# Fourier tables made and kept in the Fourier stage; the next layer's norm woven with the last out-projection

## The chip, the cores and the metric

The kernel runs on one core of a Trainium2 chip. The metric is the device time of one execution in microseconds (us). The core has a matmul engine (PE), a vector engine (DVE), a scalar engine (ACT), a general engine (POOL) and a sync engine (SP) that issues most of the DMA transfers. Each engine takes its own instructions in order; they meet through semaphores.

## The reference

Two layers of an encoder over 1040 tokens (16 learned ones and 1024 given) of width 1024. In one layer:

```
hn   = rmsnorm(h, norm_w[i])
proj = hn @ w_in[i]                      # all groups' inputs and gates
y_fft = real(fft2(u_fft, ortho)) @ fourier_w[i] * silu(g_fft)
y_pool, y_ssd, y_att = ...               # pooling, two-way state-space scan, attention
h    = h + concat(y_pool, y_fft, y_ssd, y_att) @ w_out[i]
```

The two-dimensional transform is done as matmuls with cosine and sine tables. The inner ones run over the 512 channels. Because `fourier_w` follows directly, the kernel first multiplies the channel tables with `fourier_w` (the "Fourier tables" of this text: four of 128x512 and one row of 512), and then multiplies the folded input with those.

## The kernel before

All activations stand with channels on the 128 partitions and tokens along the free dimension, in three token chunks of 348, 346 and 346. Float32 products are made from three matmuls on values split in a high part `hh` and a low part `hl` (`mm3`, L132 to L135; the split itself, L128 to L130, is an ACT copy and a DVE subtraction). A pool of 30 buffers called `big` holds almost everything of full length.

A layer runs so. `prenorm` (L156) loads the eight tiles of h from DRAM, squares them on ACT, sums them on POOL, DVE and in a matmul with ones (L175), takes the root (`rstd`), multiplies (L180) and splits (L181, L182). `att_kv` (L546) projects keys and values, and its evacuation (`qk_chunk`, L526) needs the cosine and sine tables of the rotary by DMA. `fft_tables` (L389) loads `cc`, `cn` and four blocks of `fw` by DMA; the blocks 1 and 3 come as 127 rows, since their first row is loaded apart (L402, L403). It adds and subtracts them (L407, L411), multiplies (L415, L417), copies the results out (L419) and writes them to DRAM. Then come the query projections and the four attention heads-pairs (`att_q`, `att_max`, `att_main`), with all other projections woven between them as "fill". After that come the Fourier stage (`fft_inner`, L423, `fft_outer`, L474, `fft_mix`), which loads the tables and the folded input back from DRAM and splits them, and the backward and forward scans; the out-projections of the groups (`outproj`, L320) are the fill here. Each step of `outproj` reads a 128x346 piece of the running h from DRAM (`ht`, L328), adds 12 matmuls to it (L337) and writes it to DRAM again (L338). The last out-projection runs for chunks 0 and 1 beside the forward scan and for chunk 2 alone (L1047, L1049).

`weave` and `stage` (L956, L1024) set in which order the program is written; a scheduler then orders each engine's instructions and gives the buffers out. Nearly all DMAs stand in SP's one queue, in the order in which SP issues them. `ps` gives out the PSUM banks: in the attention the ring for the out-projection ("mm") has three, the ring for small sums ("xx") one.

Of the kernel before, what the change touches and what calls it, by code (L numbers as in the profile page):

```python
# [12 lines left out]
F32R = mybir.dt.float32r  # L13
# [6 lines left out]
D = 1024  # L20
# [32 lines left out]
def hybrid_trunk(ctx: ExitStack, tc: tile.TileContext, io, out, depth=DEPTH):  # L53
# [36 lines left out]
    TE = nc.vector  # L90
    PN, PG, TB = ((2, 2, 8), ((0, 2, 4, 6), (0, 3, 6), (1, 3, 5)), 3)
# [59 lines left out]

    def vec(l, col, n=1):
        return vecs[:, l * NV + col:l * NV + col + n]


    def prenorm(l, s, src):  # L156
        h = [big() for _ in range(8)]
        hh = s.hh = [big(F32R) for _ in range(8)]
        hl = s.hl = [big(F32R) for _ in range(8)]
        for ci, (c0, cw) in enumerate(CH):  # L160
            for d in range(8):
                nc.sync.dma_start(h[d][:, c0:c0 + cw], src(d, ci))
        for ci, (c0, cw) in enumerate(CH):
            ss = ps("xx")
            n = PN[ci]
            for i in range(n):
                eng = (nc.gpsimd, nc.vector)[i % 2]
                for d in range(i, 8, n):
                    sq = chunk_tile("pl" if d == i else "pf")
                    nc.scalar.activation(sq[:, :cw], h[d][:, c0:c0 + cw], AF.Square)  # L170
                    if d == i:
                        acc = sq
                    else:
                        eng.tensor_tensor(acc[:, :cw], acc[:, :cw], sq[:, :cw], op=ALU.add)
                nc.tensor.matmul(ss[:, :cw], ones, acc[:, :cw], start=(i == 0), stop=(i == n - 1))  # L175
            rs = rstd(ss[:, :cw], cw, D)
            for d in range(8):
                t = sm()
                hi, lo = hh[d][:, c0:c0 + cw], hl[d][:, c0:c0 + cw]
                nc.vector.scalar_tensor_tensor(t[:, :cw], h[d][:, c0:c0 + cw], vec(l, V_NW + d), rs[:, :cw], op0=ALU.mult, op1=ALU.mult)  # L180
                nc.scalar.copy(hi, t[:, :cw])  # L181
                (nc.gpsimd if d in PG[ci] else nc.vector).tensor_tensor(lo, t[:, :cw], f(hi), op=ALU.subtract)  # L182
            yield
# [33 lines left out]

    def win(l, t):
        return wsplit([wraw(io["w1"][l, t, :, 4 * i:4 * i + 4]) for i in range(2)])
# [935 lines left out]
```

## Time and profile before

| | |
|---|---|
| median of 3 runs | 2183.52 us (2173.6 to 2186.84) |
| profiled execution | 2183.98 us, of it 2181.9 us span |
| PE busy | 2002.1 us, 92% |
| DVE, ACT, POOL busy | 1323.7, 1004.6, 642.0 us |
| mean granted PE clock | 0.964 |

An engine's share is an average over stages. PE is nearly full in the attention stages; what matters here is the three kinds of place where it is not: the start of each layer, the making of the Fourier tables, and the Fourier stage and the scans.

### The profile page before, as it was taken

To read this page: it belongs to the slowest core of one execution; us is meant where nothing else is said; L and a number is where in the kernel's file an instruction comes from. 1 tells how busy PE (TensorE), PEld (TensorE's weight loads), DVE (VectorE), ACT (ScalarE), POOL (GpSimd) and SP (SyncE) were. 2 spreads that over 40 slices of the span, in tenths; PEclk is the share of its full clock that TensorE was granted. 3 is DMA by queue.
4 is the path that set the end of the run, shared out by engine and by line. 5 is a ranking of instruction groups with operands and counts; after the bars stand their busy time and mean duration, and the time that the engine had idled before them with its cause. 6 is when DMAs were issued, how large, how long until landed. Compare 5 with 4: busy or idle time off the path is not lost. (4 is left out here: it accounts for less than half of the span.)

```text
span 2181.9 us, 33618 instructions
## 1 busy us (share of the span) xinstructions
PE 2002.1 (92%) x11868; PEld 1755.1 (80%) x11868; DVE 1323.7 (61%) x2614; ACT 1004.6 (46%) x2191; POOL 642.0 (29%) x642
## 2 busy tenths in 40 slices
PE   6699999989999999988976999999999999988888
PEld 5498888867899868877864988888778997878778
DVE  6373535558566355689864735256576554466996
ACT  5335254444443456346443353444435425463562
POOL 3005235135131220245220142441442304112550
PEclk9799999999999999999997999999999999999999
DMA  4321222113224478776743212121223335776666
GB/s 131 103 86 61 59 66 74 36 56 95 94 81 137 126 217 267 195 186 187 223 125 108 88 59 68 64 63 34 76 81 99 124 113 149 246 231 179 176 190 188
DMA packets 170374, 269.48 MB, mean 124 GB/s; under 512 B 21522, under 2 KB 117334, under 8 KB 170206
## 3 DMA queue, kind: packets, MB, share of 16 engines
q1 hardware_dynamic: 167550, 258.01, 39.0%
q0 software_dynamic: 2656, 9.33, 1.7%
q8 instruction: 93, 1.52, 0.3%
q14 instruction: 75, 0.61, 0.1%
HBM read 189.27 MB, written 73.77 MB: 121 GB/s over the span
## 5 line engine op out<-in xcount | busy, mean ns | idle before, releaser
L133 PE MATMUL psmm<-big,wh 128*128 128x346 f32 (+2 forms) x1920 | 639.8, 333 | 27.0 <-ACT sms L334 9.2
L134 PE MATMUL psmm<-big,wh 128*128 128x346 f32 (+2 forms) x1920 | 629.7, 328 | 7.7 <-DVE big L130 4.0
L135 PE MATMUL psmm<-big,wl 128*128 128x346 f32 (+2 forms) x1920 | 626.3, 326 | 2.0 <-DVE wl L130 2.0
L646 POOL TENSOR_TENSOR acc<-acc,pf 116x346 f32<-116x346 f32 (+4 forms) x336 | 343.9, 1048 | 531.6 <-ACT pf L637 531.5
L133 PEld LDWEIGHTS psmm<-big,wh 128*128 128x128 f32 x1920 | 367.9, 192 | 62.2 <-issue 21.7
L134 PEld LDWEIGHTS psmm<-big,wh 128*128 128x128 f32 x1920 | 368.2, 192 | 19.5 <-DVE big L130 8.4
L135 PEld LDWEIGHTS psmm<-big,wl 128*128 128x128 f32 x1920 | 368.3, 192 | 6.3 <-DVE wl L130 2.6
L130 DVE TENSOR_TENSOR wl<-wr,wh 128x512 fp32r<-128x512 f32 x232 | 182.8, 792 | 215.2 <-ACT wh L129 214.2
L129 ACT CAST wh<-wr 128x512 fp32r<-128x512 f32 (+1 forms) x236 | 145.0, 616 | 270.9 <-PE psmm L134 216.7
L133 PE MATMUL psy<-big,wh 128*128 128x346 f32 (+2 forms) x672 | 224.1, 334 | 0.0
L134 PE MATMUL psy<-big,wh 128*128 128x346 f32 (+2 forms) x672 | 223.1, 332 | 1.1 <-POOL big L182 0.7
L135 PE MATMUL psy<-big,wl 128*128 128x346 f32 (+2 forms) x672 | 219.2, 326 | 0.0
L606 DVE TENSOR_REDUCE mx<-psy 128x1 f32<-128x346 f32 (+3 forms) x272 | 132.8, 512 | 56.1 <-PE psy L605 55.4
L637 ACT ACTIVATE pf<-psy 116x346 f32<-116x346 f32 (+4 forms) x288 | 125.6, 457 | 80.3 <-PE psy L635 77.2
L656 PE MATMUL pspv<-pf,vt 116*64 116x346 f32 (+5 forms) x864 | 160.6, 463 | 0.0
L133 PEld LDWEIGHTS psy<-big,wh 128*128 128x128 f32 x672 | 129.9, 193 | 10.9 <-issue 8.8
L134 PEld LDWEIGHTS psy<-big,wh 128*128 128x128 f32 x672 | 130.0, 193 | 8.5 <-DVE big L130 2.8
L135 PEld LDWEIGHTS psy<-big,wl 128*128 128x128 f32 x672 | 130.3, 194 | 1.3 <-issue 0.8
L606 DVE TENSOR_REDUCE mx<-pssc 128x1 f32<-128x346 f32 (+3 forms) x136 | 69.9, 514 | 69.3 <-PE pssc L605 68.4
L337 DVE TENSOR_TENSOR sms<-sms,psmm 128x346 f32<-128x346 f32 (+2 forms) x128 | 65.1, 511 | 73.7 <-PE psmm L135 43.8
L656 PEld LDWEIGHTS pspv<-pf,vt 116*64 116x64 f32 (+1 forms) x864 | 58.6, 136 | 61.5 <-issue 24.0
L634 PE MATMUL psy<-big,big 128*116 128x346 f32 (+4 forms) x288 | 95.8, 334 | 8.1 <-DVE mx L606 7.2
(285 smaller groups left out, 3331.3 us busy)
## 6 DMA issues: line engine op xcount, KB each, us to landing
wr<-w SPq DMA_DIRECT2D x248, 256.0 KB
hd<-sms SPq DMA_DIRECT2D x112, 173.0 KB
sms<-hd SPq DMA_DIRECT2D x112, 173.0 KB
bb<-csd SPq DMA_DIRECT2D x40, 338.0 KB
md<-big SPq DMA_DIRECT2D x24, 520.0 KB
gd<-sms SPq DMA_DIRECT2D x64, 173.0 KB
big<-gd SPq DMA_DIRECT2D x16, 520.0 KB
big<-md SPq DMA_DIRECT2D x16, 520.0 KB
```

Source lines behind the costliest of these rows:

```text
L129: nc.scalar.copy(hi, src)
L130: nc.vector.tensor_tensor(lo, src, f(hi), op=ALU.subtract)
L133: nc.tensor.matmul(out_ps, ah, bh, start=start, stop=False)
L134: nc.tensor.matmul(out_ps, ah, bl, start=False, stop=False)
L135: nc.tensor.matmul(out_ps, al, bh, start=False, stop=stop)
L337: nc.vector.tensor_tensor(ht, ht, p[:, :cw], op=ALU.add)
L606: nc.vector.tensor_reduce(mx[:qn, q, e, ci:ci + 1], p[:qn, :cw], axis=AX.X, op=ALU.max)
L634: nc.tensor.matmul(p[:n, :cw], k1[:, k0:k0 + n], s1[e][:, cs], start=True, stop=False)
L637: nc.scalar.activation(pf[:n, :cw], p[:n, :cw], AF.Exp, scale=0.125)
L646: nc.gpsimd.tensor_tensor(accs[c0, e][:n, :cw], accs[c0, e][:n, :cw], pf[:n, :cw], op=ALU.add)
L656: nc.tensor.matmul(hold["pv"][64 * e:64 * e + 64, :cw], s.vt[:n, k, v, :], pfs[e][:n, :cw], start=(k == 0), stop=(k == len(KTS) - 1))
```

## The change

The Fourier tables are no longer made between `att_kv` and the queries but at the start of the Fourier stage, as a generator of its own, with out-projection steps between its matmuls. They are split straight from PSUM and kept in SBUF; their way through DRAM (`md["t"]`) and the loads of them in `fft_inner` are gone. `prenorm` is now written per chunk with yields. In layer 0 the weights of keys and values are loaded behind the first chunk of x and before the other two; the norms of chunks 1 and 2 are woven with the key and value projections, and 12 steps of the fill with the last of these. The last out-projection of layer 0 writes its sums into SBUF tiles (`sink`) as well as to DRAM, so that layer 1 loads no h for its norm; the norms of its chunks 0 and 1 are woven with the out-projection of chunk 2, that of chunk 2 with the key and value projections. `ssd_parts` packs three chunks in one buffer. The numbers of fill steps move accordingly (`FB`, `FN`, `FK`).

```diff
-    FB = (6, 6, 0, 1, 4, 1, 6, 9)
+    FB = (5, 5, 4, 1, 4, 1, 6, 9)
     GA = (22, 23, 22, 13)
     PS, WF = 60, 1.5
-    FN = (10, 17, 17, 17, 28)
+    FK = 3
+    FN = (9, 17, 17, 16, 27)
...
+    PN, PG = ((8, 2, 8), (2, 2, 8)), ((0, 2, 4, 6), (0, 3, 6), (1, 3, 5))
...
+    def load_h(s, src, ci):
+        c0, cw = CH[ci]
+        for d in range(8):
+            nc.sync.dma_start(s.h[d][:, c0:c0 + cw], src(d, ci))
+
+    def prenorm(l, s, ci):
+        if ci == 0:
+            s.hh = [big(F32R) for _ in range(8)]
+            s.hl = [big(F32R) for _ in range(8)]
+        c0, cw = CH[ci]
+        ss = ps("xx")
+        n = PN[l][ci]
+        for i in range(n):
+            eng = (nc.gpsimd, nc.vector)[i % 2]
+            for d in range(i, 8, n):
+                sq = sm()
+                nc.scalar.activation(sq[:, :cw], s.h[d][:, c0:c0 + cw], AF.Square)
+                if d == i:
+                    acc = sq
+                else:
+                    eng.tensor_tensor(acc[:, :cw], acc[:, :cw], sq[:, :cw], op=ALU.add)
+            nc.tensor.matmul(ss[:, :cw], ones, acc[:, :cw], start=(i == 0), stop=(i == n - 1))
+        yield
+        rs = rstd(ss[:, :cw], cw, D)
+        yield
+        for d in range(8):
+            t = sm()
+            hi, lo = s.hh[d][:, c0:c0 + cw], s.hl[d][:, c0:c0 + cw]
+            nc.vector.scalar_tensor_tensor(t[:, :cw], s.h[d][:, c0:c0 + cw], vec(l, V_NW + d), rs[:, :cw], op0=ALU.mult, op1=ALU.mult)
+            nc.scalar.copy(hi, t[:, :cw])
+            (nc.gpsimd if d in PG[ci] else nc.vector).tensor_tensor(lo, t[:, :cw], f(hi), op=ALU.subtract)
+            if d % 2:
+                yield
...
+    def win_raw(l, t):
+        return [wraw(io["w1"][l, t, :, 4 * i:4 * i + 4]) for i in range(2)]
+
     def win(l, t):
-        return wsplit([wraw(io["w1"][l, t, :, 4 * i:4 * i + 4]) for i in range(2)])
+        return wsplit(s0.raws.pop((l, t), None) or win_raw(l, t))
...
                 for k in range(4):
-                    mm3(p[:, :cw], *w[k], mh[k][:, c0:c0 + cw], ml[k][:, c0:c0 + cw], k == 0, k == 3)
+                    mm3(p[:, :cw], *w[k], part(s, 0, k, ci), part(s, 1, k, ci), k == 0, k == 3)
+                o = ht
+                if sink is not None:
+                    if len(sink) == d:
+                        sink.append(big())
+                    o = sink[d][:, c0:c0 + cw]
                 if pool:
                     t = sm("s")[:, :cw]
                     nc.scalar.copy(t, p[:, :cw])
-                    nc.gpsimd.tensor_tensor(ht, ht, t, op=ALU.add)
+                    nc.gpsimd.tensor_tensor(o, ht, t, op=ALU.add)
                 else:
-                    nc.vector.tensor_tensor(ht, ht, p[:, :cw], op=ALU.add)
-                nc.sync.dma_start(dst(d, ci)[:, -cw:], ht)
+                    nc.vector.tensor_tensor(o, ht, p[:, :cw], op=ALU.add)
+                nc.sync.dma_start(dst(d, ci)[:, -cw:], o)
                 yield
...
         nc.sync.dma_start(w2[1:2], io["fw"][l, 3, 0:1])
+        yield
...
-            o = big()[0:n, 0:512]
-            nc.scalar.copy(o, p)
-            nc.sync.dma_start(s.md["t"][i, 0:n], o)
+            if n == 128:
+                r = big(F32R)
+                s.mt.append((r[:, 0:512], r[:, 528:1040]))
+                split(*s.mt[-1], p)
+            else:
+                nc.scalar.copy(s.mn, p)
             yield
...
-            m1.append(load(s.md["t"][j], every, 512))
...
-        nc.sync.dma_start(t[one, 528:1040], s.md["t"][4, 0:1])
+        nc.scalar.copy(t[one, 528:1040], s.mn)
...
-            m2.append(load(s.md["t"][2 + j], every, 512))
...
-        m = [[big(F32R) for _ in range(4)] for _ in range(2)] if chunks[0] == 0 else s.ym
-        s.ym = m
+
+        m, t = {}, None
         for ci in chunks:
             c0, cw = s.ch[ci]
             for j in range(4):
-                split(m[0][j][:, c0:c0 + cw], m[1][j][:, c0:c0 + cw], s.y[j][:, c0:c0 + cw])
-        return m
+                for i in range(2):
+                    n = len(m) % 3
+                    if n == 0:
+                        t = big(F32R)
+                    m[i, j, ci] = t[:, 352 * n:352 * n + cw]
+                split(m[0, j, ci], m[1, j, ci], s.y[j][:, c0:c0 + cw])
+        return lambda s, i, k, ci: m[i, k, ci]
...
+    s = layer(0)
+    s.h = [big() for _ in range(8)]
+    phase["spare"] = SPARE[0]
+    load_h(s, hsrc, 0)
+    for t in (T_K, T_V):
+        s0.raws[0, t] = win_raw(0, t)
+    for ci in (1, 2):
+        load_h(s, hsrc, ci)
...
-        if TB == 0:
-            run(fft_tables(l, s))
-        next(pre)
-        if TB == 1:
-            run(fft_tables(l, s))
-        run(pre)
-        if TB == 2:
-            run(fft_tables(l, s))
-        run(att_kv(l, s))
-        if TB == 3:
-            run(fft_tables(l, s))
+        kv = att_kv(l, s)
+        if l == 0:
+            run(prenorm(l, s, 0), weave((islice(kv, 2 * PC), 2 * PC), (prenorm(l, s, 1), 6)), weave((islice(kv, 2 * PC), 2 * PC), (prenorm(l, s, 2), 6)))
+        else:
+            run(weave((islice(kv, 4 * PC), 4 * PC), (prenorm(l, s, 2), 6)))
+        s.h = None
+        run(weave((kv, 2 * PC + 2), (islice(fill, FK * PC), FK * PC)))
...
+        tabs = fft_tables(l, s)
+        next(tabs)
+        run(islice(fill2, 1))
+        stage(tabs, 5, FB[2] - 1)
         stage(fft_inner(l, s), 9, FB[1])
...
-        tail = lambda chunks: outproj(l, s, 2, lambda: ssd_parts(s, chunks), d1, hsrc, chunks)
+        sink = None if last else []
+        tail = lambda chunks: outproj(l, s, 2, lambda: ssd_parts(s, chunks), d1, hsrc, chunks, sink=sink)
...
+        rest = tail((2,))
+        if last:
+            run(rest)
+        else:
+            after = layer(l + 1)
+            after.h = sink
+            run(weave((rest, 8), (chain(prenorm(l + 1, after, 0), prenorm(l + 1, after, 1)), 12)))
+            s = after
...```

How this moves instructions is seen at three places. The first is SP's queue at the loads of the Fourier tables in layer 0; `big` tiles that read from `fw` are the blocks. Before, they stand among rotary tables (`cosT`, `sinT`), weights (`w`) and a spill (`gd`):

```order
L400 DMA big_632<-fw 128x512
L400 DMA big_633<-fw 127x512
L400 DMA big_634<-fw 128x512
L400 DMA big_635<-fw 127x512
L402 DMA big_642<-fw 1x512
L403 DMA big_642<-fw 1x512
L198 DMA wr_909<-w 128x512
L198 DMA wr_1100<-w 128x512
L234 DMA gd_693<-sms_752 128x348
L539 DMA smn_889<-cosT 128x346
L540 DMA smn_890<-sinT 128x346
```

Now they stand at the end of the attention, among the last load of the pooled group (`md`) and the pieces of h that the first out-projection reads (`xT`) and writes (`hd`):

```order
L420 DMA big_7551<-fw 127x512
L330 DMA sms_7277<-md_125 128x346
L343 DMA sms_7287<-xT 128x348
L343 DMA sms_7304<-xT 128x346
L343 DMA sms_7321<-xT 128x346
L420 DMA big_7552<-fw 128x512
L420 DMA big_7553<-fw 127x512
L358 DMA hd_5727<-sms_7287 128x348
L343 DMA sms_7350<-xT 128x348
L358 DMA hd_5728<-sms_7304 128x346
L422 DMA big_7560<-fw 1x512
L358 DMA hd_5729<-sms_7321 128x346
```

So the same 127-row loads now have the out-projection's traffic behind them in the queue, in place of the rotary tables and the queries' weights.

The second place is DVE at the same point, where the blocks are added (L428, L432), the out-projection's sums are taken (L357) and the attention's last divisions are made (L693 to L695):

```order
L357 TENSOR_TENSOR sms_7321<-sms_7321,psmm_7323 128x346
L130 TENSOR_TENSOR wl_8034<-wr_8031,wh_8033 128x512
L428 TENSOR_TENSOR big_7551<-big_7552,big_7553 128x512
L357 TENSOR_TENSOR sms_7350<-sms_7350,psmm_7352 128x348
L428 TENSOR_TENSOR big_7553<-big_7552,big_7553 128x512
L432 TENSOR_TENSOR big_7550<-big_7550,big_7551 128x512
L432 TENSOR_TENSOR big_7551<-big_7550,big_7551 128x512
L432 TENSOR_TENSOR big_7552<-big_7552,big_7553 128x512
L357 TENSOR_TENSOR sms_7367<-sms_7367,psy_7369 128x346
L693 TENSOR_TENSOR smn_7474<-smn_7473,psxx_7470 128x346
```

The third addition, L428 into `big_7551`, needs the second 127-row block (`big_7553`); the division L693 stands behind it.

The third place is PE at the tables themselves. Before, a table's matmuls stand together, with queries' matmuls (`psy_715`) around them:

```order
L415 MATMUL psy_653<-big_632,big_629 128x512
L417 MATMUL psy_653<-big_642,big_629 128x512
L415 MATMUL psy_659<-big_633,big_629 128x512
L571 MATMUL psxx_626<-ct,big_343 112x128
L134 MATMUL psy_715<-big_104,wh_711 128x348
```

Now an out-projection step of 12 matmuls stands between them (`psmm_7603`, `psy_7630` and so on):

```order
L135 MATMUL psmm_7603<-big_7228,wl_7598 128x348
L437 MATMUL psy_7618<-big_7551,big_7547 128x512
L437 MATMUL psxx_7623<-big_7552,big_7547 128x512
L133 MATMUL psy_7630<-big_7225,wh_7597 128x346
L134 MATMUL psy_7630<-big_7229,wh_7597 128x346
L135 MATMUL psy_7630<-big_7225,wl_7598 128x346
```

The number of table matmuls is the same, eight a layer.

## Rows read from the trace of the kernel before

**Rows 1.** The page's first part: busy time, share of the span, instructions.

```profile
PE 2002.1 (92%) x11868; PEld 1755.1 (80%) x11868; DVE 1323.7 (61%) x2614; ACT 1004.6 (46%) x2191; POOL 642.0 (29%) x642
```

**Rows 2.** Windows: length, busy PE, PEld, DVE, ACT, POOL; clock, DMA share, GB/s.

```profile
66.98:100.98 34.00, 17.19 (x33) 7.48 (x32) 11.73 (x24) 7.62 (x16) 2.02 (x2) 0.60 0.27 92
1162.99:1193.77 30.78, 11.55 (x19) 3.26 (x18) 12.35 (x24) 7.21 (x15) 2.30 (x2) 0.61 0.26 85
755.00:862.00 107.00, 97.81 (x556) 80.58 (x557) 62.31 (x109) 66.01 (x111) 19.58 (x22) 0.98 0.80 245
1837.00:1935.00 98.00, 91.52 (x531) 77.09 (x531) 57.68 (x104) 62.15 (x103) 18.22 (x20) 0.98 0.82 256
```

**Rows 3.** Timeline of PE, layer 0: start, length, instruction [idle before and releaser].

```profile
25.27 0.50 PE L133 MATMUL psmm<-big,wh 128*128 128x348 f32 x1
...
99.08 1.02 PE L415 MATMUL psy<-big,big 128*1 128x512 f32 x2
100.03 1.01 PE L417 MATMUL psy<-big,big 2*1 2x512 f32 x2
...
105.76 0.85 PE L533 MATMUL psxx<-smq,ct 128*128 128x348 f32 x2
```

**Rows 4.** Timeline of SP's queue, layer 1: the issues of the table loads.

```profile
1152.42 7.28 SPq L400 DMA_DIRECT2D big<-fw  x4
1159.75 10.22 SPq L402 DMA_DIRECT2D big<-fw  x1
```

**Rows 5.** Windows of one microsecond inside these loads.

```profile
1178.00:1179.00 1.00, 0.00 (x0) 0.00 (x0) 0.00 (x0) 0.00 (x0) 0.00 (x0) 0.50 0.07 24
```

**Rows 6.** Timeline of DVE, layer 1: the third addition of the blocks.

```profile
1179.34 0.69 DVE L407 TENSOR_TENSOR big<-big,big 128x512 f32<-128x512 f32 x1 [8.83 <-DMA big<-fw]
```

**Rows 7.** Timeline of PE from the last out-projection of layer 0 into layer 1.

```profile
1086.13 0.33 PE L133 MATMUL psmm<-big,wh 128*128 128x346 f32 x1
...
1112.99 1.52 PE L175 MATMUL psxx<-pl,ones 128*128 128x346 f32 x2 [8.02 <-POOL pl L174]
...
1122.47 0.74 PE L175 MATMUL psy<-pl,ones 128*128 128x346 f32 x2
...
1195.76 0.72 PE L533 MATMUL psxx<-smq,ct 128*128 128x332 f32 x2
```

**Rows 8.** Windows: a full attention stretch, then key and value projections of both layers.

```profile
1250.00:1300.00 50.00, 50.00 (x315) 45.82 (x314) 17.24 (x26) 26.16 (x60) 25.83 (x28) 1.00 0.16 55
25.27:66.98 41.71, 35.73 (x190) 32.19 (x188) 33.02 (x60) 25.10 (x56) 13.31 (x11) 0.92 0.29 88
1119.67:1162.99 43.32, 40.19 (x224) 34.93 (x222) 33.89 (x60) 26.58 (x60) 13.25 (x13) 1.00 0.24 73
```

**Rows 9.** Timeline of ACT at the start: squares of chunk 0, then its root.

```profile
8.85 1.64 ACT L170 ACTIVATE pf<-big 128x348 f32<-128x348 f32 x4 [0.48 <-DMA big<-xT]
...
13.69 0.55 ACT L139 ACTIVATE smn<-psy,epst 128x348 f32<-128x348 f32 x1 [0.61 <-PE psy L175]
```

**Rows 10.** Timeline of DVE at the start: the first products of the norm.

```profile
17.93 2.06 DVE L180 SCALAR_TENSOR_TENSOR smn<-big,vecs,smn 128x348 f32<-128x348 f32 x4
```

**Rows 11.** Groups of the first 100 us: total busy us, mean ns, idle before.

```profile
L180 DVE SCALAR_TENSOR_TENSOR smn<-big,vecs,smn 128x346 f32<-128x346 f32 (+1 forms) x24 | 16.3, 727 | 0.0
...
L181 ACT CAST big<-smn 128x346 fp32r<-128x346 f32 (+1 forms) x24 | 11.2, 477 | 4.7 <-DVE smn L180 4.6
...
L130 DVE TENSOR_TENSOR wl<-wr,wh 128x512 fp32r<-128x512 f32 x9 | 7.4, 842 | 0.0
```

**Rows 12.** Windows of 22 us from the end of the pooled group's loads on.

```profile
757.00:779.00 22.00, 21.03 (x109) 14.37 (x109) 14.85 (x24) 12.58 (x28) 9.14 (x9) 1.00 0.70 200
1837.00:1859.00 22.00, 22.00 (x119) 14.76 (x118) 15.70 (x22) 13.62 (x30) 13.84 (x13) 1.00 0.80 232
```

**Rows 13.** Timeline of SP's queue: the pooled group's last load, layer 1.

```profile
1837.11 0.32 SPq L315 DMA_DIRECT2D sms<-md  x1
```

**Rows 14.** Timeline of PE, layer 1: the attention's last sums.

```profile
1859.80 0.80 PE L665 MATMUL psxx<-acc,ones 116*64 116x346 f32 x2 [0.53 <-POOL acc L646]
```

More of the change, by code (lines that the diff above doesn't have):

```diff
@@ L150, in hybrid_trunk @@
         pass
+    s0 = S()
+    s0.raws = {}
     def vec(l, col, n=1):
         return vecs[:, l * NV + col:l * NV + col + n]
[L156 to L183, printed above, removed]
@@ L308, in gates, with whole @@
         return g
+    def whole(m):
+        return lambda s, i, k, ci: m[i][k][:, s.ch[ci][0]:sum(s.ch[ci])]
     def load_mixed(s, key):
@@ L316, in load_mixed, with outproj @@
                 split(m[0][k][:, c0:c0 + cw], m[1][k][:, c0:c0 + cw], t[:, :cw])
-        return m
-    def outproj(l, s, g, mixed, src, dst, chunks=(0, 1, 2), pool=False):
-        mh, ml = mixed()
+        return whole(m)
+    def outproj(l, s, g, mixed, src, dst, chunks=(0, 1, 2), pool=False, sink=None):
+        part = mixed()
         for d in range(8):
@@ L406, in fft_tables @@
             x = 2 * (i % 2)
-            TE.tensor_tensor(b[i], a[x], a[x + 1], op=(ALU.add, ALU.subtract)[i // 2])
+            nc.vector.tensor_tensor(b[i], a[x], a[x + 1], op=(ALU.add, ALU.subtract)[i // 2])
         for i, op in enumerate((ALU.add, ALU.subtract, ALU.subtract, ALU.add)):
@@ L515, in fft_mix @@
         g = s.gf
-        s.fm = [], []
+        fm = [], []
+        s.fm = whole(fm)
         for d in range(4):
@@ L977, in by_rows, with layer @@
         return lambda d, ci: x[d * 128:d * 128 + 128, max(CH[ci][0] - off, 0):sum(CH[ci]) - off]
-    hsrc = by_rows(io["xT"])
+    def layer(l):
+        s = S()
+        s.ch = [(NM, CH[0][1] - NM)] + CH[1:] if l == depth - 1 else CH
+        s.out = slice(s.ch[0][0], L)
+        s.md, s.s1, s.q2, s.xbc, s.z, s.gd, s.h = {}, {}, {}, {}, [], {}, []
+        return s
+    hsrc = by_rows(io["xT"])
+    s = layer(0)
[6 more added lines that the diff above has]
+        load_h(s, hsrc, ci)
     for l in range(depth):
-        s = S()
         last = l == depth - 1
-        s.ch = [(NM, CH[0][1] - NM)] + CH[1:] if last else CH
-        s.out = slice(s.ch[0][0], L)
-        s.md, s.s1, s.q2, s.xbc, s.z, s.gd = {}, {}, {}, {}, [], {}
         scope = ExitStack()
@@ L1048, in hybrid_trunk @@
         scope.close()
-        run(tail((2,)))
+        rest = tail((2,))
[6 more added lines that the diff above has]
+            s = after
 def _rnd12(x):
```

14 lines of the change are left out of this document (5 added, 9 removed).

## The prediction

> **What bounds the kernel now.** I read the busy shares first, then windows over the whole span, then the PE timeline where the windows show holes. PE is busy 92% of the span [rows 1], and in the attention stretches it is full: 315 matmuls in 50.00 us, 0.159 us each [rows 8]. So time can come only out of the remaining holes or be lost in new ones. The windows show three kinds. At the start, the first projection stands at 25.27 [rows 3]. Around the making of the Fourier tables PE is busy 17.19 of 34.00 us in layer 0 and 11.55 of 30.78 in layer 1, at a granted clock of 0.60 and 0.61, so near its lower level of 1.2 GHz [rows 2]. Between the layers there is an idle stretch of 8.02 us with slow matmuls around it [rows 7]. The Fourier stage is another matter: PE is busy 97.81 of 107 us and 91.52 of 98 us, with the DMA engines at 0.80 and 0.82 [rows 2]. There is little room in it on either resource.
>
> **Why the tables cost so much.** In layer 1 the four block loads are issued from 1152.42 on. SP is held 7.28 us in these and 10.22 us in the next one [rows 4], and the addition that needs the last block starts at 1179.34, having waited 8.83 us for DMA [rows 6]: 27 us for 1 MB. Inside the hold all that moves is 24 GB/s at a DMA share of 0.07 [rows 5], one engine of 16. The blocks that do this are the two of 127 rows. Everything behind them in SP's queue is held too, rotary tables and weights among it, and so PE.
>
> The Trainium skill says why (DMA: Bandwidth & Descriptors, "Why a DMA increments its semaphore by 16 and not by 1"): the number of engines used is the largest up to 16 that divides the slowest dimension, and it gives 127 partitions as a case of one engine. The share of 0.07 agrees. It speaks against this change, which keeps both loads as they are and moves them to where the queue is fuller; the second rival below is what that would do.
>
> **The sum, part by part.** As a common mark I take the matmul that sums the squares of the first query chunk (L533): 105.76 in layer 0 [rows 3], 1195.76 in layer 1 [rows 7]. What PE has to do before it can be counted from the instruction order.
>
> *Layer 0 up to the mark.* The squares of chunk 0 end at 10.49 (8.85 + 1.64) [rows 9]. Chunk 0 now gets eight matmuls with ones in place of additions; the last follows one such matmul later, 0.74 [rows 7]. From the root to the first product took 13.69 to 17.93, 4.24 us [rows 9, 10]. A product of 0.73 and a cast of 0.48 follow [rows 11]. The first projection then stands at 16.7, with its weights there, since they are loaded behind the first chunk. Behind it come 205 split matmuls and 9 transposes at 0.159 [rows 8], 34.0 us, and 10 matmuls with ones and 3 of L533's kind at 0.74, 9.6 us. The projections waited 41.71 - 35.73 = 6.0 us in this stretch [rows 8]; I keep that, since the norms still feed them. The mark falls at 66.3: **39 us won**, between 32 (14 us of waits) and 45 (none). The fill of 72 matmuls that is now woven in costs nothing: it is work taken from later stages, whose numbers in FN fall by 1 in three places.
>
> *Layer 1 up to the mark.* The last out-projection starts at 1086.13 [rows 7]. From there PE has 308 split matmuls and 9 transposes, 50.4 us, and 13 of the others, 9.6: 1146.1. The waits of the projections were 3.1 us [rows 8]. DVE now has its whole norm here as well: 111 instructions up to the mark in the order, 24 products at 0.73, 15 weight splits at 0.84 [rows 11] and 72 others at 0.52 [rows 10], 67 us, nearly PE's 60 and 10 for the woven fill. I add 4 us for that. Mark at 1153.2: **43 us won**, between 35 and 47. The h that is no longer loaded costs the queue nothing any more; its 8 us of idle PE are in this sum.
>
> *The tables' matmuls in the Fourier stage.* Eight a layer, and a pair of instructions follows the next by 100.03 - 99.08 = 0.95 us at the full clock [rows 3]: 7.6 us, 15 in both layers. PE idles 9.2 and 6.5 us in these stages [rows 2], a hole here and there, so I count all of it. The splits of the tables only change their source (PSUM for SBUF); four loads and four stores of 256 KB go, so the stage has as many block loads as table loads before. The eight additions of 0.69 [rows 6], 5.5 us a layer, lie in DVE's idle time, 44.7 and 40.3 us [rows 2].
>
> *The block loads in the Fourier stage.* They need buffers that the last projection frees, so they are issued with the pooled group's last load, 1837.11 in layer 1 [rows 13]. If they take 27 us again, the last block is there at 1864 and the first table matmul can start 3 us later, 1867. PE reaches that place at about 1861: the attention's last sums end at 1860.6 [rows 14], one out-projection step of 12 matmuls (1.9) is now fewer ahead of them, and one stands behind. Until then PE has work that needs none of the held transfers (22.00 of 22 us busy, 21.03 in layer 0 [rows 12]): exponentials, and out-projection steps whose sums wait in three PSUM banks. So 6 us of the 27 are seen. DVE stands behind the second block too (the third L428), with the attention's division behind it; it comes free at the same time, so it adds nothing. What was not moved in these 22 us, at 200 and 232 GB/s [rows 12] some 4.4 and 5.1 MB, must follow in a stage whose DMA share is 0.8; a fifth of 98 us is free, about as much as was lost. I take 3 us for what collides (the folded input stands behind all this in the queue). That makes **9 us a layer**, with bounds of -3 (the weaving fills old holes) and 27 (nothing covers).
>
> Sum: 39 + 43 - 15 - 18 = 49 us less. The profiled execution took 2183.98 us, 0.5 above the median, so **2135 us**.
>
> **The rivals.**
> *All covered.* The attention's tail hides the blocks whole, the stage only gets the 15 us: 2184 - 82 + 15 = 2117. For it: PE is full in that window [rows 12] and the loads may be issued a little earlier than I say. Against it: the out-projection's pieces are behind them in the queue.
> *Nothing covered.* One-engine transfers hold SP, the pieces of h don't come, the three banks fill, and PE stands 27 us a layer: 2184 - 82 + 15 + 54 = 2171. For it: that is what happened before, with PE idle for 19 of 31 us [rows 2]. Against it: PE had no other work there and here it has. By the skill's rule alone, each block would take 254 KB at 24 GB/s, 10.6 us, 21 a layer.
> *DVE bounds the weaving.* It has 67 us of work to PE's 70 in the seam, and stands in order behind casts of ACT. If the norm feeds the projections no sooner than before, some 10 us a layer are lost: 2155.
> *The holes stay.* The queries' weights or rotary tables are late for another reason and a third of the table holes remains: 20 us, and 2155 too.
> *Slower.* SP's hold and its backlog both show: 27 us a layer, then 18 to 21 us to move 4.4 and 5.1 MB at the stage's 245 GB/s [rows 2], with 7.6 of matmuls. 2 x 54 = 108 against 82: 2210. It decides from where the stage's DMA share has no free fifth left and the out-projection runs no step ahead of its loads.
>
> **How the numbers follow.** Forecast 0.44 (its own range 2121 to 2150), all covered 0.20, DVE 0.12, holes 0.06, nothing covered 0.12, slower 0.06. The range of 2106 to 2163 takes in the first four with their bounds and the lower part of the fifth; some 0.16 lies outside. A measurement of this kernel can tell about 1% from no change, 22 us: faster means under 2162. That takes in the first four nearly whole and a fifth of the fifth, 0.83; within 1% is the rest of these and half of the last, 0.14; slower by over 1% is 0.03.
>
> **What would show it.** First projection near 17 us and first L533 for a query near 78 in layer 0 (the woven fill adds 11 to the mark). No stretch of PE at the lower clock in the first 110 us of a layer. In the Fourier stage, the 24 GB/s windows are there again, with PE busy through most of them and a wait of a few us ahead of the first table matmul. The forecast is wrong where that wait is over 15 us, where the stage grows by more than 25 us, or where PE's holes between the layers move to the out-projection of chunk 2.

## The result and the profile after

The change takes 2172.11 us (median of 20 runs, 2166.86 to 2178.49) where the kernel before takes 2184.62: a ratio of 0.9944, interval 0.9932 to 0.9956. That is 12.5 us less, a quarter of the 49 that were forecast, and outside the range. The profiled executions differ by 11.4 us in their spans.

The page of the changed kernel, span and part 1, against [rows 1]:

```profile
span 2170.5 us, 33606 instructions
PE 2006.2 (92%) x11880; PEld 1760.7 (81%) x11880; DVE 1335.7 (62%) x2611; ACT 1011.5 (47%) x2185; POOL 645.4 (30%) x639
```

First the start and the seam. These are rows of PE's timeline of the changed kernel: the first projection, and the matmul that sums the squares of the first query chunk (L557, L533 before) in layers 0 and 1.

```profile
17.59 0.66 PE L133 MATMUL psmm<-big,wh 128*128 128x348 f32 x1 [5.42 <-ACT big L188]
83.94 0.75 PE L557 MATMUL psxx<-smq,ct 128*128 128x348 f32 x2
1169.12 0.72 PE L557 MATMUL psxx<-smq,ct 128*128 128x332 f32 x2
```

They stood at 25.27, 105.76 and 1195.76 [rows 3, 7]. The marks come 21.8 and 26.6 us earlier, and by count 71 and 64 more split matmuls (L133 to L135; 11.3 and 10.2 us at 0.159) now lie ahead of them, about as many as the 72 of the woven fill. The holes around the tables and at the seam are gone: between 1080 us and the mark of layer 1 PE's longest wait is 2.3 us, where it was 8.0 and 19.2.

Now the Fourier stage. These windows of the changed kernel give their length in us, busy time by engine, granted clock, DMA share and GB/s: the stretch up to the mark, and the 50 us in each layer in which the attention ends and the tables are made.

```profile
50.00:84.00 34.00, 31.41 (x185) 28.43 (x184) 22.78 (x42) 20.39 (x45) 5.46 (x5) 1.00 0.39 120
720.00:770.00 50.00, 37.49 (x168) 24.35 (x166) 22.81 (x36) 15.96 (x38) 18.83 (x18) 0.86 0.47 135
1790.00:1840.00 50.00, 38.61 (x177) 26.19 (x178) 25.19 (x39) 16.30 (x39) 18.29 (x17) 0.86 0.48 145
```

PE, which had 17.19 of 34.00 us of work ahead of the mark [rows 2], now has 31.41. But in the Fourier stage it idles 12 us in each layer and runs part of the rest at a clock of 0.5, the lower of its two levels. What happens there is read queue by queue. SP's issues in layer 0 (start, us held):

```profile
729.74 0.75 SPq L420 DMA_DIRECT2D big<-fw  x2
730.60 4.81 SPq L330 DMA_DIRECT2D sms<-md  x1
735.51 1.84 SPq L343 DMA_DIRECT2D sms<-xT  x3
737.41 2.33 SPq L420 DMA_DIRECT2D big<-fw  x2
```

The first two blocks go out, the second of them with 127 rows, then the last piece of the out-projection's mixed input (md), three pieces of xT, then the other two blocks. DVE meanwhile:

```profile
733.32 1.86 DVE L130 TENSOR_TENSOR big<-sms,big 128x346 fp32r<-128x346 f32 x2 [0.56 <-ACT big L129]
744.82 0.69 DVE L428 TENSOR_TENSOR big<-big,big 128x512 f32<-128x512 f32 x1 [9.64 <-DMA big<-fw]
...
758.02 0.85 DVE L428 TENSOR_TENSOR big<-big,big 128x512 f32<-128x512 f32 x1 [8.82 <-DMA big<-fw]
```

So the 127-row blocks land near 745 and 758, 15 and 28 us after the first issue: the 27 us of before [rows 4, 6], as forecast. For most of that time the DMA engines move what [rows 5] showed (windows of 2 us: clock, DMA share, GB/s); from 736 to 740 and from 748 to 754, when SP gets other issues out, it is more:

```profile
734.00:736.00 2.00, 1.00 0.07 26
744.00:746.00 2.00, 0.50 0.07 24
```

ACT and PE in the same stretch:

```profile
745.23 0.48 ACT L129 CAST big<-sms 128x346 fp32r<-128x346 f32 x1 [8.34 <-DMA sms<-md]
```

```profile
736.56 1.38 PE L680 MATMUL pspv<-pf,vt 116*64 116x346 f32 x8
745.76 1.37 PE L133 MATMUL psmm<-big,wh 128*128 128x346 f32 x2 [7.82 <-ACT big L129]
...
763.72 1.42 PE L689 MATMUL psxx<-acc,ones 116*64 116x346 f32 x4 [3.29 <-DVE smn L693]
...
768.70 1.69 PE L437 MATMUL psy<-big,big 128*128 128x512 f32 x2
```

PE does not first stop at the tables. It stops 8 us after the blocks' issue, at an out-projection matmul whose input is the md piece. That piece was issued behind the 127-row block and lands with it: SP held its issue for 4.81 us, and it was cast only 9.8 us after that. Layer 1 repeats this: PE waits 7.5 us for ACT's cast and 3.1 for DVE.

### The profile page after: what moved, and what is told of

Same layout as the page of the kernel before. It is cut to its first block, busy times and chain, and to the rows that moved or that the text cites. A ratio compares the mean times of both kernels' runs of the same rounds, so it can differ in the third digit from the quotient of the medians.

```text
span 2170.5 us, 33606 instructions
## 1 busy us (share of the span) xinstructions
PE 2006.2 (92%) x11880; PEld 1760.7 (81%) x11880; DVE 1335.7 (62%) x2611; ACT 1011.5 (47%) x2185; POOL 645.4 (30%) x639
## 3 DMA queue, kind: packets, MB, share of 16 engines
q8 instruction: 93, 1.52, 0.3%
## 5 line engine op out<-in xcount | busy, mean ns | idle before, releaser
L133 PE MATMUL psmm<-big,wh 128*128 128x346 f32 (+2 forms) x1920 | 646.3, 337 | 43.9 <-ACT big L129 18.8
L134 PE MATMUL psmm<-big,wh 128*128 128x346 f32 (+2 forms) x1920 | 634.4, 331 | 5.5 <-DVE big L130 2.2
L135 PE MATMUL psmm<-big,wl 128*128 128x346 f32 (+2 forms) x1920 | 628.4, 328 | 0.3 <-DVE wl L130 0.3
L670 POOL TENSOR_TENSOR acc<-acc,pf 116x346 f32<-116x346 f32 (+4 forms) x336 | 344.6, 1050 | 542.6 <-ACT pf L661 542.2
L133 PEld LDWEIGHTS psmm<-big,wh 128*128 128x128 f32 x1920 | 371.1, 193 | 88.5 <-issue 30.0
L134 PEld LDWEIGHTS psmm<-big,wh 128*128 128x128 f32 x1920 | 371.2, 193 | 16.7 <-DVE big L130 5.2
L135 PEld LDWEIGHTS psmm<-big,wl 128*128 128x128 f32 x1920 | 372.1, 194 | 3.4 <-DVE wl L130 0.8
L130 DVE TENSOR_TENSOR wl<-wr,wh 128x512 fp32r<-128x512 f32 x232 | 183.2, 793 | 216.9 <-ACT wh L129 215.6
L129 ACT CAST wh<-wr 128x512 fp32r<-128x512 f32 (+1 forms) x236 | 145.2, 616 | 259.0 <-PE psmm L134 207.9
L133 PE MATMUL psy<-big,wh 128*128 128x346 f32 (+2 forms) x672 | 223.6, 333 | 2.7 <-ACT wh L129 2.3
L134 PE MATMUL psy<-big,wh 128*128 128x346 f32 (+2 forms) x672 | 218.7, 325 | 0.2 <-DVE big L130 0.2
L135 PE MATMUL psy<-big,wl 128*128 128x346 f32 (+2 forms) x672 | 217.7, 324 | 0.0
L680 PE MATMUL pspv<-pf,vt 116*64 116x346 f32 (+5 forms) x864 | 162.8, 464 | 0.0
L630 DVE TENSOR_REDUCE mx<-psy 116x1 f32<-116x346 f32 (+3 forms) x272 | 132.9, 510 | 32.8 <-PE psy L629 31.5
L133 PEld LDWEIGHTS psy<-big,wh 128*128 128x128 f32 x672 | 128.8, 192 | 14.6 <-issue 8.4
L134 PEld LDWEIGHTS psy<-big,wh 128*128 128x128 f32 x672 | 128.5, 191 | 4.2 <-DVE big L130 2.8
L135 PEld LDWEIGHTS psy<-big,wl 128*128 128x128 f32 x672 | 128.5, 191 | 0.8 <-issue 0.5
L680 PEld LDWEIGHTS pspv<-pf,vt 116*64 116x64 f32 (+1 forms) x864 | 57.8, 136 | 60.0 <-issue 24.6
L668 POOL TENSOR_TENSOR acc<-pf,pf 116x346 f32<-116x346 f32 (+2 forms) x48 | 53.7, 1138 | 145.2 <-ACT pf L661 145.2
```

The lines of the kernel that those rows point to most:

```text
L129: nc.scalar.copy(hi, src)
L130: nc.vector.tensor_tensor(lo, src, f(hi), op=ALU.subtract)
L133: nc.tensor.matmul(out_ps, ah, bh, start=start, stop=False)
L134: nc.tensor.matmul(out_ps, ah, bl, start=False, stop=False)
L135: nc.tensor.matmul(out_ps, al, bh, start=False, stop=stop)
L630: nc.vector.tensor_reduce(mx[:qn, q, e, ci:ci + 1], p[:qn, :cw], axis=AX.X, op=ALU.max)
```

## The experiments

Times are medians; the ratio is to the kernel before as measured beside each run, with its interval. That kernel's median differed by some 6 us from one set to the next, so the ratios compare better across sets than the times. "127" behind a heading means that the two loads of 127 rows are kept, "full" that both blocks are loaded with 128.

**Full rows in the change.**

```diff
         for i in range(4):
-            if i % 2:
-                nc.vector.memset(a[i][0:1], 0.0)
-            nc.sync.dma_start(a[i][i % 2:128], io["fw"][l, i, i % 2:128])
+            nc.sync.dma_start(a[i], io["fw"][l, i])
+            if i % 2:
+                nc.vector.memset(a[i][0:1], 0.0)
```

> The change, but blocks 1 and 3 of the Fourier weights are loaded with all 128 rows, and row 0 is set to zero behind the load; nothing else differs. Theory A (the two loads of 127 rows run on one DMA engine, DVE stands in order behind them at the additions of L428 with the out-projection's additions behind it, and PE runs dry): from about 720 us to the end of the Fourier stage the change loses 30 to 32 us a layer, of which 7.6 are the tables' matmuls, so 22 to 24 a layer come back: 2172 - 46 = 2126, between 2112 and 2140; the first table matmul of layer 0 falls from 768 to near 750. Theory B (the stage is too full on DMA and DVE for any added work, and the blocks' loads only stand in the same place): at most 6 us a layer come back, 2160 to 2172.

Measured 2144.46, ratio 0.9843 (0.9825 to 0.9861): faster than the change by 28 us by the medians and 22 by the ratios, more than theory B's 12 and less than theory A's 46. The issues of SP, and what ACT and PE do later in the stage:

```profile
728.06 0.42 SPq L418 DMA_DIRECT2D big<-fw  x1
729.20 0.32 SPq L330 DMA_DIRECT2D sms<-md  x1
729.61 0.38 SPq L418 DMA_DIRECT2D big<-fw  x1
```

```profile
733.07 0.48 ACT L129 CAST big<-sms 128x346 fp32r<-128x346 f32 x1
...
773.05 1.28 ACT L311 ACT_TABLE_LOAD   x1 [5.45 <-DMA z<-gd]
...
775.61 0.61 ACT L129 CAST big<-big 128x521 fp32r<-128x521 f32 x1
```

```profile
776.27 0.42 PE L133 MATMUL psxx<-big,big 128*36 128x512 f32 x1 [4.16 <-ACT big L129]
```

The md piece is cast 4 us after its issue, not 15, and PE is busy 48.42 us of 720 to 770. (The edit moved the order too: the piece now goes out between the first block and the second, no longer behind both. The run with 112 and 15 rows, below, keeps it behind the second.) From the mark to the stage's last matmul this kernel loses 14.8 and 10.8 us a layer against the kernel before in equal work, the change 28.9 and 23.4: the 127-row loads are 14.1 and 12.6 of that. The rest is not theirs, and the last rows show one part of it: the cast of the folded input stands on ACT behind the load of z.

**Full rows in the kernel before.** The same edit.

> The kernel before with the same edit of the two loads alone. Theory A (the 127-row loads made most of the hole around the tables, where PE stood idle 17 us in layer 0 and 19 in layer 1 and then ran at the lower clock): the four blocks land in some 8 us instead of 27, about 15 us a layer come back, 2184 - 30 = 2154, between 2140 and 2170. Rival (the holes are made by the queries' weights and rotary tables or by the norm, and the loads only stand there): 2175 to 2186.

Measured 2133.95, ratio 0.9795 (0.9777 to 0.9814): 46 us, beyond theory A, and faster than the change with full rows. The windows over the tables' stretch in both layers, where [rows 2] had PE busy for 17.19 of 34.00 and 11.55 of 30.78 us:

```profile
60.00:95.00 35.00, 33.67 (x164) 26.83 (x165) 21.82 (x46) 19.45 (x40) 3.87 (x3) 0.95 0.43 144
1120.00:1152.00 32.00, 30.14 (x148) 22.30 (x148) 25.30 (x49) 20.58 (x45) 5.45 (x5) 1.00 0.59 179
```

The holes around the tables were made by these two loads almost alone.

**Weaving alone (127).** The tables in their old place and through DRAM, with the old FB; all else as in the change.

```diff
...
+        run(fft_tables(l, s))
         phase["spare"] = SPARE[1]
...
-        tabs = fft_tables(l, s)
-        next(tabs)
-        run(islice(fill2, 1))
-        stage(tabs, 5, FB[2] - 1)
```

> The change without its move of the tables: they are made behind the keys and values, stored and loaded again as before, and the fill counts of the Fourier stage are the old ones; the norm woven with the projections and with the out-projection, and h kept on chip, stay. Theory A (the move won about 25 us a layer at the start and lost 32 in the Fourier stage): the weaving alone is worth 68 - 50 = 18 us or a little more, 2150 to 2170. Theory B (moving the tables is a loss, the weaving carries all the gain): below 2140. Rival C (the weaving is worth nothing without the move, because the tables' hole swallows it): 2175 to 2186.

Measured 2161.55, ratio 0.9926 (0.9907 to 0.9945): 19 us less by the medians, theory A's 18. By the intervals the change (0.9932 to 0.9956) is no faster than this.

**Tables moved alone (127).** The kernel before with the tables in the Fourier stage, the change's FB, and no weaving.

> The kernel before with the tables made in the Fourier stage and kept on chip, with the change's fill counts there; the norm, the load of h and the seam between the layers as before. Theory A: 25 us a layer won at the start, 32 lost in the Fourier stage: 2184 + 14 = 2198, between 2180 and 2205. Theory B: the move is a small gain by itself, 2150 to 2175.

Measured 2181.2, ratio 1.0014 (1.0001 to 1.0026), at the lower end of theory A: the move by itself gains nothing. The same stop is there (PE's waits from 715 to 820, total, times, longest):

```profile
PE psmm L133 <- ACT big L129: 7.1, 2, 6.9
```

**The additions on POOL (127).**

```diff
-            nc.vector.tensor_tensor(b[i], a[x], a[x + 1], ...
+            nc.gpsimd.tensor_tensor(b[i], a[x], a[x + 1], ...
...
-            nc.vector.tensor_tensor(a[i], b[x], b[x + 1], op=op)
+            nc.gpsimd.tensor_tensor(a[i], b[x], b[x + 1], op=op)
```

> The change with its 127-row loads as they are, and the eight additions of L428 and L432 on POOL instead of DVE. Full rows gave back 28 us; the question is through which engine the slow loads were seen. Theory DVE (the additions that need the late blocks stand in DVE's order ahead of the out-projection's additions and splits, and PE waits for those): DVE runs on, PE's waits of 7.8 and 3.3 us ahead of the tables go, and what is left is the wait of the first table matmul for the second block (758) and four additions of some 1.1 us on POOL, near 763 instead of 768: 5 to 8 us a layer, 2172 - 13 = 2159, between 2154 and 2164. Theory queue (SP is held by the 127-row loads and the out-projection's pieces come late): nothing changes, 2168 to 2176.

Measured 2182.36, ratio 1.0012 (1.0000 to 1.0025): 10 us slower than the change (15 by the ratios), which neither theory had. PE's rows, and DVE's sum of the out-projection:

```profile
745.86 1.26 PE L133 MATMUL psmm<-big,wh 128*128 128x346 f32 x2 [7.15 <-ACT big L129]
...
770.51 2.28 PE L689 MATMUL psxx<-acc,ones 116*64 116x346 f32 x4 [8.55 <-POOL acc L670]
```

```profile
745.90 0.52 DVE L357 TENSOR_TENSOR sms<-sms,psmm 128x348 f32<-128x348 f32 x1 [9.42 <-DMA sms<-xT]
```

DVE is free of the blocks and PE waits as before for the cast of the md piece, so DVE's order did not make this wait; it is theory queue's. DVE's own row shows more of it: the first xT piece, which SP issued 5 us behind the block, also arrives only when the block does. The second wait moved with the additions: the attention's sums now stand behind them on POOL.

**The out-projection's steps ahead of the additions (127).**

```diff
-        run(islice(fill2, 1))
-        stage(tabs, 5, FB[2] - 1)
+        run(islice(fill2, FB[2]))
+        run(tabs)
```

> The change with the four out-projection steps of the tables' stretch all ahead of the additions, and the five tables behind them without steps between: an order alone. Theory DVE: three more steps of 1.9 us stand in DVE's order ahead of the wait for the first block, so PE has 5.7 us of work in its idle 7.8, and the tables lose the steps between them, some 1 to 2 us: 4 us a layer, 2172 - 8 = 2164, between 2158 and 2170. Theory queue: the steps wait for their pieces as before, 2170 to 2180.

Measured 2176.43, ratio 0.9990 (0.9976 to 1.0005), within theory queue's range, with the same wait of 7.4 us for ACT's cast. PE stops in the same half-done step: it needs the late piece itself, and the steps put forward stand behind it in PE's order.

**Where the loads are issued from (127).** From ACT as below, and from POOL with `nc.gpsimd` in that place.

```diff
-            nc.sync.dma_start(a[i][i % 2:128], ...
+            (nc.sync, nc.scalar)[i % 2].dma_start(a[i][i % 2:128], ...
```

> The change with its two 127-row loads issued from ACT's queue instead of SP's; rows, engines and everything else as they were. In the change a piece of the mixed input (L330) that SP issued right behind the first slow load landed only with it, and PE waited 7.8 us for it, though its other fifteen sixteenths had long moved. Theory ring (what SP issues later stands behind the slow load on the same DMA engine): the piece lands at once and that wait goes; what DVE's additions hold up remains: 4 to 8 us a layer back, 2172 - 12 = 2160, between 2154 and 2165. Theory SP hold (the wait is the issue that was held): the same, less than 2160 to 2166. Theory engine (the one engine is simply full, whoever fills it): no change, 2168 to 2176.

From ACT: 2172.32, ratio 0.9958 (0.9943 to 0.9972), no change: the time of the third theory. But its mechanism is not what the rows show. SP, ACT, DVE and PE of that run:

```profile
728.66 0.36 SPq L330 DMA_DIRECT2D sms<-md  x1
730.68 0.51 ACTq L420 DMA_DIRECT2D big<-fw  x1
730.71 2.74 SPq L343 DMA_DIRECT2D sms<-xT  x3
```

```profile
733.94 0.48 ACT L129 CAST big<-sms 128x346 fp32r<-128x346 f32 x1 [0.63 <-DMA sms<-md]
```

```profile
737.90 0.52 DVE L357 TENSOR_TENSOR sms<-sms,psy 128x346 f32<-128x346 f32 x1 [0.81 <-DMA sms<-xT]
745.81 1.33 DVE L428 TENSOR_TENSOR big<-big,big 128x512 f32<-128x512 f32 x1 [7.40 <-DMA big<-fw]
...
757.76 1.90 DVE L428 TENSOR_TENSOR big<-big,big 128x512 f32<-128x512 f32 x3 [10.20 <-DMA big<-fw]
```

```profile
762.88 1.42 PE L689 MATMUL psxx<-acc,ones 116*64 116x346 f32 x4 [13.30 <-DVE smn L693]
```

The md piece no longer has a 127-row block ahead of it in SP's queue (ACT issues that 2 us later); it is cast 5.3 us after its issue, and PE's first wait is gone. PE runs on and is stopped by the second mechanism instead, 13.3 us where it was 3.3: the attention's division stands on DVE behind the additions. The blocks land when they did, and DVE stands for them. So does SP: its waits show 8.3 and 9.3 us that end with the landings of these blocks, although ACT issued them, so the out-projection's later pieces and stores stood as well. The Trainium skill (DMA: Bandwidth & Descriptors, "Queues, rings and completion order") says that SP and ACT have a ring each on every engine and that an engine takes a ring's descriptors in order. The piece that landed with the block in the change agrees with the second half; for the first, the first two xT pieces that SP issued from 730.71 on, behind ACT's load, were in use by 737.90, 8 us before that load landed.

> The same two loads issued from POOL. If what POOL issues is spread over the engines in another way than SP's loads, the blocks land in a few us as with full rows, and the time is 2140 to 2150. If 127 rows stay on one engine whoever issues them: 2158 to 2176 as in the run before it. Worse than 2176 if the wait for the buffers stands ahead of the attention's sums on POOL.

From POOL: 2148.80, ratio 0.9850 (0.9827 to 0.9872), nearly full rows. POOL's issue and the addition that needs the first of the two blocks:

```profile
728.03 1.11 POOL L420 DMA_DIRECT2D big<-fw  x2
```

```profile
736.42 3.87 DVE L428 TENSOR_TENSOR big<-big,big 128x512 f32<-128x512 f32 x3
```

**The same rows in two parts.** 112 rows and 15, from SP.

```diff
+            cuts = (1, 113, 128) if i % 2 else (0, 128)
+            for r0, r1 in zip(cuts, cuts[1:]):
+                nc.sync.dma_start(a[i][r0:r1], io["fw"][l, i, r0:r1])
```

> The change with its two slow loads cut in two: rows 1 to 112 and rows 113 to 127, so 112 and 15 rows in place of 127, the same rows into the same partitions. Theory A (a load of 127 rows is served by one DMA engine because 127 has no divisor up to 16 but one): the parts go over 16 and 15 engines, and the time is that of full rows, 2144, between 2138 and 2150. Rival (what is slow is the destination that begins at partition 1, or the row 0 that is written beside it): it stays at 2172.

Measured 2140.53, ratio 0.9802 (0.9786 to 0.9819): as full rows or a little better. SP's first issues, the first block and 112 rows of the second ahead of the md piece, and ACT's cast of that piece:

```profile
727.90 0.90 SPq L422 DMA_DIRECT2D big<-fw  x2
728.91 0.36 SPq L330 DMA_DIRECT2D sms<-md  x1
```

```profile
734.95 0.48 ACT L129 CAST big<-sms 128x346 fp32r<-128x346 f32 x1
```

The piece stands in the same place of the queue as in the change, and ACT does not wait for it. Neither the first partition nor the row beside it made the loads slow; the count 127 did. The rule of the Trainium skill that the prediction cited (DMA: Bandwidth & Descriptors, "Why a DMA increments its semaphore by 16 and not by 1") gives 112 rows sixteen engines and 15 rows fifteen, and this run's time agrees. The same section of the Trainium skill says that some copies issued from GpSimd (POOL here) are spread over the engines by rounding up, 127 rows among them; the POOL run agrees, with its blocks in use 8.4 us after their issue.

**The folded input first (full).** The loads and splits of the folded input (md["r"]) ahead of the tables' matmuls.

```diff
...
+        s.fr = []
+        for j in range(4):
+            s.fr.append(fold_load(s, j))
         s.mt, s.mn = [], big()[0:1, 0:512]
...
-            fe.append(load(s.md["r"][2 * j], every, HALF + 1))
+            fe.append(s.fr[2 * j])
...
```

> The change with full rows, and the four loads and splits of the folded input in the program ahead of the tables' matmuls. With full rows the Fourier stage still took 16 us a layer more than before it was moved, 7.6 of them the tables' matmuls. In that run ACT stood 5.45 us for the load of z (L947) with the cast of the folded input behind it, and PE 4.2 us for that cast. If this order makes the rest, 4 to 8 us a layer go: 2144 - 10 = 2134, between 2128 and 2138. If the rest is a full stage, the wait turns up elsewhere: 2140 to 2148.

Measured 2139.98, ratio 0.9794 (0.9773 to 0.9814), against 0.9843 (0.9825 to 0.9861) for the change with full rows: 4 us by the medians, 10 by the ratios. This lies between the two ranges. PE's wait of 4.16 us for that cast is gone. Part of the rest was this order.

**Weaving with full rows, tables in their old place.** As it is; without FK's fill (FN as before); and with the start of layer 0 unwoven too, so that only the seam is woven.

> The weaving without the move of the tables (they are made behind the keys and values and go through DRAM as before), and the two blocks loaded with all 128 rows. From the runs so far: the full rows gave 46 us to the kernel before, the weaving 19 with the tables' hole in it. If the two add: 2180 - 46 - 19 = 2115. If the hole that the full rows close is the same that the weaving closed (part of the 19): down to 2134. Theory A expects 2105 to 2120, since the weaving's own part is the first projection and the seam, which the loads did not touch.

> The weaving with full rows and the tables in their old place (2133 so far, no better than full rows alone), without the fill that the change weaves with the last keys and values: FK is gone and FN has its old numbers. By the marks that run was 5 us ahead in equal work at the first attention products of layer 0 and 4 behind at the attention's end. If the fill that was taken out of the attention costs that: 5 to 8 us a layer, 2133 - 10 = 2123, between 2115 and 2128. If not: 2130 to 2137.

> As the run before it, and the start of layer 0 unwoven: all three chunks of the norm ahead of the keys and values. The seam between the layers stays woven, h on chip. If the woven start is worth what its first projection gains (17.6 instead of 25.3, some 5 to 8 us), this is slower than the run before by that; if the projections only waited for the later chunks instead, within 2 us of it.

Measured 2132.73, 2132.80 and 2133.50; ratios 0.9780 (0.9763 to 0.9796), 0.9767 (0.9750 to 0.9783), 0.9765 (0.9743 to 0.9786). All stand within a few us of full rows alone (0.9777 to 0.9814): the holes that the two edits close are in the main the same, and theory A's 2105 to 2120 was wrong. The fill that was taken out of the attention costs nothing that shows, and the woven start is worth nothing that shows. A fourth one, with the tables woven among the keys and values, gave 2132.81, where 2100 to 2125 had been expected. So of the weaving's 19 us beside the 127-row loads all but some 1 to 6 were those loads' hole.

What the seam still wins shows at the mark of layer 1, 1143.52 with only the seam woven and 1150.59 in full rows alone. Part of it is given back ahead of it. The last SSD norm of layer 0, in full rows alone and in the run with only the seam woven:

```profile
1051.55 1.52 PE L935 MATMUL psy<-sms,ones 128*128 128x346 f32 x2 [2.23 <-DVE sms L932]
```

```profile
1056.54 1.52 PE L956 MATMUL psy<-sms,ones 128*128 128x346 f32 x2 [5.75 <-DVE sms L953]
```

Of these 5.0 us, 4.3 are there already at the last matmul of the Fourier stage: 816.80 and 821.06, with the same 3139 split matmuls behind it.

**Do the buffers of h cause this?** Full rows alone, with eight big buffers held through the out-projection of chunks 0 and 1 in layer 0; and two tiles of their own for the SSD's ecd loads, beside the woven seam and beside full rows alone. All three also load the two blocks with 128 rows, which is not shown here.

```diff
...
+            if held is not None:
+                held.append(big())
+                nc.gpsimd.memset(held[d][0:1, 0:1], 0.0)
...
```

```diff
...
-            e = vr(big())
+            e = vr(phase["p"].tile([128, 8 * QC], F32, name=nm("ecd"), tag="ecd", bufs=2))
...
```

> The kernel before with full rows (2134) in which, in layer 0 only, the out-projection of chunks 0 and 1 takes eight of the 30 big buffers one after the other and holds them to its end, as the change does for h; nothing is kept in them. In the woven runs the loads of L896 (big<-ecd) for the last SSD chunk of layer 0 are issued at 1048 and 1051 instead of 1028 and 1032, and that layer's last norm comes 5 to 10 us later than with full rows alone. If the buffers that h holds cause it: 2134 + 7, between 2138 and 2145. If it is the order of the norm's work or DVE's load: 2130 to 2137.

> Seam woven, start unwoven, full rows (2133.5), and the SSD's ecd loads get two tiles of their own in the SSD's pool instead of big buffers. If the held buffers cost 5 to 10 us at the end of layer 0: 2126, between 2121 and 2129. If not: 2131 to 2136.

> The control to the run before it: the kernel before with full rows (2134) and the same two tiles for the ecd loads. If these help only where h holds buffers: 2131 to 2136. If they help anywhere: below 2130.

Measured 2135.78, 2140.93 and 2143.60; ratios 0.9806 (0.9789 to 0.9824), 0.9828 (0.9815 to 0.9842), 0.9842 (0.9828 to 0.9855). Held buffers change nothing (that layer's last norm stays at 1052), and own tiles make both kernels slower. The theory falls. The run with held buffers differs from full rows alone only behind the Fourier stage, and its last matmul there stands at 819.19: some 2 of the 5 us are what two executions differ by. Where the rest comes from stays open, but most of it is not in the last SSD chunk.

## Why the prediction was wrong, point by point

I keep a ledger in equal work, from PE's marks of the two profiled executions; with one execution of each kernel, a term can be off by a few us. Work is counted in split matmuls that PE had begun, at 0.159 us each. The change had 71 and 64 more behind it at the L557 marks (11.3 and 10.2 us), and 45 more in either layer at the last matmul of the Fourier stage (7.2 us; that matmul moved from 843.56 to 846.46 and from 1917.96 to 1911.73). The numbers of fill put only two out-projection steps more, 24 matmuls, ahead of that place; the rest is the order that PE took.

*The start* was forecast at 39 us and measures 33 (21.8 + 11.3). The first projection came at 17.59 for 16.7, the mark at 83.94 for 77.7 with its fill. The mechanism was right; behind the first projection PE stood idle for 7 us, not 6, and a dozen of its matmuls went at the lower clock, 0.29 us apart instead of 0.16. That is over half of the 6 us; the rest is not taken apart.

*The seam and the tables' hole of layer 1* were forecast at 43 and measure 40: the last SSD norm of layer 0 moved from 1075.09 to 1078.38, with as many split matmuls behind it, and the mark by -26.6 - 10.2. Right. These are the norms:

```profile
1075.09 0.85 PE L935 MATMUL psy<-sms,ones 128*128 128x346 f32 x2 [2.94 <-DVE sms L932]
```

```profile
1078.38 1.52 PE L959 MATMUL psxx<-sms,ones 128*128 128x346 f32 x2 [6.44 <-DVE sms L956]
```

They say something that the sum left out: from the Fourier stage to here layer 0 loses 7.5 us. With full rows it loses 7.3 us, so it is not the block loads; what makes it stays open.

*The tables' matmuls*, 7.6 us a layer: nothing contradicts them, and no run took them apart from the rest.

*The block loads* are the step that the runs show to have failed: "Until then PE has work that needs none of the held transfers" and "So 6 us of the 27 are seen". The durations were right (28 us for 27, 24 to 26 GB/s), the cover was not. PE's order holds an out-projection matmul 8 us behind the issue, and its input was queued behind the slow block. I had counted PE's busy time in that stretch of the kernel before [rows 12] as cover, where no slow block stood ahead of the md pieces. A second sentence failed with it: that DVE "comes free at the same time, so it adds nothing". The run with loads from ACT takes away the first wait, and the second one appears in full, 13.3 us. Seen were 14.1 and 12.6 us a layer instead of 9. The stage as a whole grew by 28.9 us in layer 0, past the 25 at which I had called the forecast wrong, and by 23.4 in layer 1.

*What I had at nothing* weighs more than that miss of 9 us. With full rows the stage still lost 14.8 and 10.8 us a layer from the mark on, of which the matmuls are 7.6. Of the remaining 3 to 7, the order of the folded input's cast behind z is shown (2 to 5 us a layer came back without it). The rest is not taken apart. I had taken the swap of four loads and four stores as neutral; that the tables' casts and additions are in the way of a stage in which PE waits on ACT and DVE is argued, not shown. The ends of the layers, 7.5 and 2.0 us, were not in the sum at all.

The sum: 33.1 + 40.1 won, 28.9 + 23.4 lost in the two stretches that hold the Fourier stages, 7.5 lost at the end of layer 0 and 2.0 at that of layer 1, is 11.4. Forecast were 82 won and 33 lost. So the 38 us that are missing fall into four parts of about the same size: 9 in the start and the seam, 9 in the block loads, 10 in the rest of the Fourier stages, 9.5 at the ends of the layers. Only the second is explained by runs, and the third in part. Of the rivals "nothing covered" (2171) came nearest in time, but that is in part luck: the pieces of h did come late, yet PE had stopped before it needed them, SP was held 4.81 us at most, and the three banks of PSUM were not what stopped PE.

What the sum missed above all is in the run with full rows in the kernel before and in the three woven runs: the profile showed that these loads made the holes, I wrote so, and then costed a change that moves the holes instead of the edit that closes them.

## What to carry to other kernels

When a profile names the transfer that makes a hole, mend the transfer first: an edit of two loads a layer gave 46 us, and the whole weaving on top of it nothing that these runs can tell. Before a slow transfer is moved under other work, follow each queue past it: count as cover only the work whose own inputs are issued ahead of it and whose instructions stand ahead of its users on every engine. Two waits on one late block hide each other: moving the queue took the first away and the time did not change.

## What the runs showed of the hardware

A transfer of 173 KB that SP issued right behind a load of 127 rows was cast 14.6 us after its issue began, when that load had landed; in the same place behind 112 rows it was cast after 6.0 us, and ACT had not waited for it. SP itself was held 4.81 us in that issue, and 0.36 us in the same issue behind 112 rows. The same 127 rows were ready for the addition within 8.4 us when POOL issued them, and only after some 15 when SP or ACT did. And 112 and 15 rows in two loads were no slower than 128 in one.
